# Layer 1's output projection in seven quarter products in place of eight, in a decoder step on one core

## The chip, the core and the metric

The kernel is one launch on one core of a Trainium2 chip. The core has five engines that each work through an instruction list of their own, in order: TensorE (PE: matmuls and transposes), VectorE (DVE), ScalarE (ACT), GpSimd (POOL) and SyncE (SP, which issues most of the DMAs). They wait for one another by semaphores. The metric is the device time of the launch in microseconds, the median of several runs; lower is better.

## The reference

One inference step of a trunk with two layers: 1040 prompt tokens (16 meta tokens and 1024 more) and 8 sample tokens, model width 1024, fp32. Layer 0 mixes by gated linear attention, layer 1 by differential attention over 8 heads of width 128; behind each mixer stand an output projection, a residual with a layer norm, an MLP of hidden width 4096 with a squared ReLU, and a residual with a layer norm again. What the change touches is the end of layer 1's mixer:

```
def post_norm(x, f, g, b):
    return layer_norm(DEEPNORM_ALPHA * x + f, g, b)

def diff_output(o, g_sub, lam_init, w_out, dtype):
    B, T = o.shape[:2]
    o = rms_norm(o, g_sub) * (1.0 - lam_init)
    return o.reshape(B, T, DIFF_HEADS * DIFF_DV).astype(dtype) @ w_out

def sq_relu_mlp(x, w1, w2):
    h = jax.nn.relu(x @ w1)
    return (h * h) @ w2
```

That is, a matrix of 1024 tokens x 1024 head columns times w_out (1024 x 1024), added to the residual stream, normalized, and given to the MLP. The meta and sample tokens go a small separate way.

## The kernel before

**Products in fp32.** An fp32 operand is split in two parts, hi and lo (`split`, L202 a cast on ACT, L203 a subtraction on DVE), and a product is three matmuls, hi x hi, lo x hi, hi x lo (`mm3`, L206 to L208). The parts of weights are named whi and wlo, those of tokens XH and XL, or two XH buffers. Weight parts come from a load into raw, rw or RW, a cast on ACT and a subtraction on POOL (L193 and L194, or L1585 and L1586).

**Layer 1's attention and w_out.** The attention writes each head's output into Y (tokens x columns). The "back" of a head transposes probabilities (L1318), copies them (ACT L1320), multiplies with the values (L1323), and evicts (ACT L1412). When four token tiles of a head are done and scaled (L1337), `o_fm` transposes them on PE (L1343) and makes the parts XH (ACT L1344) and XL (DVE L1345) of the features-first operand. As those heads finish, their space in Y is loaded with the scaled residual (`Y<-xres`, L1442, eight loads on SP). `w_out` then goes through 4 units of 256 output columns x 8 token tiles; each tile sums 8 k x 3 matmuls of 256 columns, two tiles to a PSUM bank, and DVE adds a bank to Y (L1022). Some of this work fills gaps of the attention's tail.

**Statistics and norm.** `normalize` takes the tiles that w_out yields: statistics (DVE L1045), their sum (L1049, L1053), a power on POOL (L1054), the shift (DVE L1058), and the scaled copy on ACT (L1060). After four tiles `to_fm` transposes them (PE L1071) and evicts them, scaled by the norm's weights, into XR (DVE L1075, ACT L1077), the MLP's tokens. The residual of the MLP, Y times a constant times ln_mix_g, is made by L1700 from `grow`, a row that lies in the buffer RP (load L1453).

**The MLP of layer 1.** Its up and down products are already in the seven-product form of quarters, once for each quarter g of the hidden width. `chip_operand` makes a token operand: a difference of two quarters where the table says so (DVE L1560 into RX), then the splits, into one of two XH buffers in turn. `weight_operand` makes a weight operand: loads (SP L1582), for a difference an accumulating DMA from POOL's queue (L1584), cast and subtraction. `up_tile` adds tiles of 258 columns into HF, `down_tile` tiles of 512 columns into RP (the running sum, L1659 and a copy L1663) and Y (L1659). The tables UP_X, UP_W, DOWN_H and DOWN_W say which quarters enter a product; "run" is the operand of an earlier product, still in RX or RW, carried on.

**What sets the order.** The program's text is not the order of the engines. The tile framework places each engine's instructions by a modelled timeline, in the priority of the program's text, and sets the semaphores. So an edit can move instructions that it doesn't name, and each engine then keeps that list at run time, whatever comes late.

Of the kernel before, what the change touches and what calls it, by code (L numbers as in the profile page):

```python
# [11 lines left out]
F32 = mybir.dt.float32  # L12
# [9 lines left out]
P = 128  # L22
D = 1024
# [91 lines left out]
def hybrid_step(ctx, tc, A, dbg=None, upto=9):  # L115
# [1222 lines left out]

    def o_fm(h, c):
        cs = slice(512 * c, 512 * c + 512)  # L1340
        ps = axt()
        for i in range(4):
            TE.transpose(ps[:, i * P : (i + 1) * P], Yt[:, 4 * c + i, h * P : (h + 1) * P], ident)  # L1343
        S.activation(XH[:, h, cs], ps, AF.Copy, scale=gs)  # L1344
        V.scalar_tensor_tensor(XL[:, h, cs], ps, gs, XH[:, h, cs].bitcast(F32), ALU.mult, ALU.subtract)  # L1345
# [106 lines left out]
    grow = RP[:, 0:2, :].rearrange("p a n -> p (a n)")  # L1452
    dma(grow, A["ln_mix_g"][1:2].broadcast_to([P, D]))  # L1453

# [35 lines left out]

    stats = ln_stats(hp)
    normalize(w_out(A["diff_w_out"][0], True, samples()), stats, lambda c: to_fm(c, 2, xr))
# [48 lines left out]

    count = [0, 0]
    loads = []
    sides = []

    def chip_operand(terms, quarter, n, tmp):


        parts = [x.rearrange("p k n -> p (k n)")[:, : 4 * n] for x in XH.t[count[0] % 2]]
        count[0] += 1  # L1550
        hi, lo = (x.rearrange("p (k n) -> p k n", n=n) for x in parts)
        rv, tv = (x[:, : 4 * n].rearrange("p (k n) -> p k n", n=n) for x in (RX, tmp))
        for j in (0, 2):
            b = slice(j, j + 2)
            x = quarter(*terms[0])[:, b]
            if len(terms) > 1:

                y = rv[:, b] if terms[1] == "run" else quarter(*terms[1])[:, b]
                out = (tv if terms[1] != "run" else rv)[:, b]
                V.tensor_tensor(out, x, y, op=ALU.subtract)  # L1560
                x = out
            split(hi[:, b], lo[:, b], x)
        return hi, lo

    def weight_operand(terms, quarter, side=None):

        hi, lo = (wsp.tile([P, 2048], F32R, name=n).rearrange("p (k n) -> p k n", n=512) for n in ("whi", "wlo"))
        run = terms[0] == "run"
        own = []

        def src(q, k):
            w, r0, c0 = quarter(*q)
            return w[r0 + k * P : r0 + (k + 1) * P, c0 : c0 + 512]

        for k in range(4):
# [171 lines left out]
```

## Time and profile before

| | us |
|---|---|
| median of 3 runs | 2814.77 |
| the runs | 2809.8 to 2817.36 |
| profiled execution, its time | 2803.96 |
| profiled execution, its span | 2802.2 |

In the profiled execution the granted TensorE clock was 0.993 of full speed, and 1.00 in the stages spoken of here. PE is busy 2715.8 us of the span, 97%. Rows of a timeline have the start, the duration, the engine, the line, the operation and its operands (out<-in); in brackets behind it stands how long the engine was idle before, and what released it. Durations of matmuls overlap, so their spacing is read from the starts. In a row of a group the numbers behind the bar are the busy time of the group, the mean of one in ns, and the idle time ahead of it. Windows are in us from the start of the span.

### The profile page before, as it was taken

To read this page: it belongs to the slowest core of one execution; us is meant where nothing else is said; L and a number is where in the kernel's file an instruction comes from. 1 tells how busy PE (TensorE), PEld (TensorE's weight loads), DVE (VectorE), ACT (ScalarE), POOL (GpSimd) and SP (SyncE) were. 2 spreads that over 40 slices of the span, in tenths; PEclk is the share of its full clock that TensorE was granted. 3 is DMA by queue.
4 is the path that set the end of the run, shared out by engine and by line. 5 is a ranking of instruction groups with operands and counts; after the bars stand their busy time and mean duration, and the time that the engine had idled before them with its cause. 6 is when DMAs were issued, how large, how long until landed. Compare 5 with 4: busy or idle time off the path is not lost.

```text
span 2802.2 us, 52241 instructions
## 1 busy us (share of the span) xinstructions
PE 2715.8 (97%) x19849; PEld 2233.8 (80%) x19849; DVE 1954.0 (70%) x3045; ACT 1096.4 (39%) x2233; POOL 1105.1 (39%) x744
## 2 busy tenths in 40 slices
PE   8988999999999999999999999999999999999997
PEld 5866767987777777777798988776899889797985
DVE  5466463668877777777677730887648888979788
ACT  4324363152231221221241112777535546355553
POOL 2142112243443343433234222100026677687774
PEclk9999999999999999999999999999999999999998
DMA  7565654735889898888658995122144455555584
GB/s 234 168 231 194 215 183 170 267 96 183 311 317 335 307 351 307 315 319 305 235 197 302 363 365 169 55 61 74 37 120 91 102 146 115 141 121 122 132 187 91
DMA packets 275624, 562.81 MB, mean 201 GB/s; under 512 B 23510, under 2 KB 144412, under 8 KB 271276
## 3 DMA queue, kind: packets, MB, share of 16 engines
q1 hardware_dynamic: 256076, 522.75, 54.1%
q0 software_dynamic: 19296, 36.71, 8.1%
q8 instruction: 156, 2.56, 0.4%
q14 instruction: 96, 0.79, 0.1%
HBM read 533.00 MB, written 29.52 MB: 201 GB/s over the span
## 4 chain that ended last, share of the span: by engine, by line
PE 74%; DVE 8%; ACT 4%; DMA 3%; issue 2%; POOL 1%; SPq 0%; DVEq 0%; POOLq 0%; ACTq 0%
PE mmt L206 17%; PE mmt L207 17%; PE mmt L208 17%; PE smt L952 4%; PE axt L206 3%; PE axt L207 3%; PE axt L208 3%; PE smt L1323 2%; ACT as L1301 2%; DVE pg L911 1%; PE prt L1297 1%; DMA swt<-in_mlp_w 1%; PE axt L1318 1%; DMA rw<-in_mlp_w 1%; PE smt L686 1%
## 5 line engine op out<-in xcount | busy, mean ns | idle before, releaser
L194 POOL TENSOR_TENSOR wlo<-raw,whi 128x512 fp32r<-128x512 f32 x252 | 364.4, 1459 | 730.6 <-ACT whi L193 599.6
L206 PE MATMUL mmt<-whi,XH 128*128 128x256 f32 (+1 forms) x1760 | 524.6, 300 | 1.3 <-DVE ast L1299 0.9
L207 PE MATMUL mmt<-wlo,XH 128*128 128x256 f32 (+1 forms) x1760 | 522.2, 298 | 0.4 <-POOL wlo L194 0.4
L206 PE MATMUL mmt<-XH,whi 128*128 128x512 f32 (+1 forms) x1216 | 434.2, 358 | 6.6 <-DVE Y L1022 3.0
L208 PE MATMUL mmt<-XH,wlo 128*128 128x512 f32 (+1 forms) x1216 | 432.0, 356 | 0.0
L208 PE MATMUL mmt<-whi,XL 128*128 128x256 f32 x1536 | 431.7, 284 | 0.0
L193 ACT CAST whi<-raw 128x512 fp32r<-128x512 f32 x252 | 150.5, 620 | 579.3 <-PE mmt L208 189.6
L206 PEld LDWEIGHTS mmt<-whi,XH 128*128 128x128 f32 x1760 | 330.7, 189 | 39.1 <-issue 24.3
L912 DVE TENSOR_REDUCE sc<-pg 128x16 f32<-128x1024 f32 x256 | 308.2, 1211 | 70.5 <-POOL pg L911 68.1
L207 PEld LDWEIGHTS mmt<-wlo,XH 128*128 128x128 f32 x1760 | 332.2, 189 | 17.5 <-issue 6.8
L207 PE MATMUL mmt<-XL,whi 128*128 128x512 f32 x768 | 306.9, 400 | 0.0
L911 DVE TENSOR_TENSOR pg<-pg,qb 128x1024 f32<-128x1024 f32 x192 | 262.7, 1375 | 57.9 <-DMA pg<-in_cache_k 46.8
L208 PEld LDWEIGHTS mmt<-whi,XL 128*128 128x128 f32 x1536 | 288.3, 189 | 4.4 <-issue 3.8
L206 PEld LDWEIGHTS mmt<-XH,whi 128*128 128x128 f32 x1216 | 229.0, 189 | 50.8 <-issue 7.5
L911 POOL TENSOR_TENSOR pg<-pg,qb 128x1024 f32<-128x1024 f32 x64 | 165.4, 2585 | 253.1 <-DMA pg<-in_cache_k 168.4
L208 PEld LDWEIGHTS mmt<-XH,wlo 128*128 128x128 f32 x1216 | 229.4, 189 | 36.4 <-issue 3.7
L206 PE MATMUL mmt<-whi,HH 128*128 128x512 f32 x512 | 204.6, 401 | 4.9 <-DVE Y L1136 3.4
L208 PE MATMUL mmt<-whi,HL 128*128 128x512 f32 x512 | 203.9, 398 | 0.0
L207 PE MATMUL mmt<-wlo,HH 128*128 128x512 f32 x512 | 203.4, 397 | 0.0
L1586 POOL TENSOR_TENSOR wlo<-RW,whi 128x512 fp32r<-128x512 f32 x96 | 166.1, 1767 | 58.1 <-ACT whi L1585 58.0
L1586 POOL TENSOR_TENSOR wlo<-rw,whi 128x512 fp32r<-128x512 f32 x92 | 156.8, 1778 | 79.1 <-ACT whi L1585 78.8
L207 PEld LDWEIGHTS mmt<-XL,whi 128*128 128x128 f32 x768 | 145.2, 189 | 38.4 <-issue 7.2
(438 smaller groups left out, 5707.8 us busy)
## 6 DMA issues: line engine op xcount, KB each, us to landing
pg<-in_cache_k SPq DMA_DIRECT2D x256, 512.0 KB
pg<-in_cache_v SPq DMA_DIRECT2D x256, 512.0 KB
raw<-in_mlp_w SPq DMA_DIRECT2D x164, 256.0 KB
swt<-in_mlp_w SPq DMA_DIRECT2D x32, 1024.0 KB
rw<-in_mlp_w SPq DMA_DIRECT2D x116, 256.0 KB
RW<-in_mlp_w POOLq DMA_DIRECT2D x96, 256.0 KB, 5.8
swt<-in_gla_w_in SPq DMA_DIRECT2D x12, 1024.0 KB
swt<-in_diff_w_in SPq DMA_DIRECT2D x12, 1024.0 KB
```

The costliest lines, as they stand in the source:

```text
L193: S.copy(hi[:, c], raw)
L194: G.tensor_tensor(lo[:, c], raw, hi[:, c].bitcast(F32), op=ALU.subtract)
L206: TE.matmul(ps, ah, bh, start=first, stop=False)
L207: TE.matmul(ps, ah, bl, start=False, stop=False)
L208: return TE.matmul(ps, al, bh, start=False, stop=last)
L686: TE.matmul(ps[o : o + TS, :], lhs[:, k + 2 * j + i, :], ts[j][:, i, c * 512 : (c + 1) * 512], start=k == 0 and j == 1, stop=k == nk - 4 a ...
L911: eng.tensor_tensor(pg, pg, qb, op=ALU.mult)
L912: return V.tensor_reduce(sc[:, n, :], pg.rearrange("p (h d) -> p h d", d=64), op=ALU.add, axis=AX.X).ins
L952: m = TE.matmul(acc[i * TS : i * TS + 16, :256], w[r, n, :], pg[r, i * 256 : (i + 1) * 256], start=n == 0, stop=n == NPG).ins
L1301: S.activation(sc_[:, m, :W], sc_[:, m, :W], AF.Exp, bias=mns[:, m : m + 1], scale=-1.0, accum_out=l[:, m : m + 1])
L1323: TE.matmul(out, at, v, start=j == 0, stop=j == t + 1)
L1586: G.tensor_tensor(lo[:, k, :], t, hi[:, k, :].bitcast(F32), op=ALU.subtract)
```

## The change

`w_out` of layer 1 becomes `w_out_1`: seven products of quarters (512 tokens or columns a side) in the order 1, 2, 5, 6, 3, 7, 4, by the tables DOWN_H and DOWN_W that the MLP's down product uses, with `chip_operand`, `weight_operand` and `down_tile`, which move up in the text for it. Each product has 4 token tiles, each of 4 k x 3 matmuls of 512 columns, so 336 matmuls stand for 768. `o_fm` keeps whole fp32 columns, OF0 and OF1, with one eviction for each four tiles (ACT for even heads, DVE for odd ones); the parts are made by `chip_operand`. The first two products' weights use the buffers raw alone. RP now holds running sums of w_out, so the load of `grow` into it moves behind w_out. Layer 0's w_out stays as it was. The line numbers shift: L1346 is the heads' transpose now, L1447 the residual's load, L1511 the difference, L1536 to L1540 the weights, L1558 and L1562 the sums and the copy of `down_tile`, L1702 the load of grow, and L1732 the multiplication that was L1700.

```diff
     def o_fm(h, c):
-        cs = slice(512 * c, 512 * c + 512)
+        if c == len(OF):
+            OF.append(cp.tile([P, NB, TH], F32, name="OF%d" % c, tag="XL%d" % c))
         ps = axt()
         for i in range(4):
             TE.transpose(ps[:, i * P : (i + 1) * P], Yt[:, 4 * c + i, h * P : (h + 1) * P], ident)
-        S.activation(XH[:, h, cs], ps, AF.Copy, scale=gs)
-        V.scalar_tensor_tensor(XL[:, h, cs], ps, gs, XH[:, h, cs].bitcast(F32), ALU.mult, ALU.subtract)
+        if h % 2:
+            V.tensor_scalar(OF[c][:, h, :512], ps, gs, None, ALU.mult)
+        else:
+            S.activation(OF[c][:, h, :512], ps, AF.Copy, scale=gs)
...
-    grow = RP[:, 0:2, :].rearrange("p a n -> p (a n)")
-    dma(grow, A["ln_mix_g"][1:2].broadcast_to([P, D]))
...
     def weight_operand(terms, quarter, side=None):
...
+        plain = len(seen) < 2
+        seen.append(0)
...
             if run or (len(terms) > 1 and terms[-1] != "new"):
                 t = RW[:, k, :]
             else:
                 count[1] += 1
-                t = wrp.tile([P, 512], F32, name="raw") if count[1] % 7 in (0, 3) else rawt()
+                t = wrp.tile([P, 512], F32, name="raw") if plain or count[1] % 7 in (0, 3) else rawt()
...
+    def w_out_1():
+
+        side = samples()
+        wo = A["diff_w_out"][0]
+
+        def operands(i):
+            left = chip_operand(DOWN_H[i], lambda c, k: OF[c][:, 4 * k : 4 * k + 4, :512], 512, RX)
+            return left, weight_operand(DOWN_W[i], lambda k, u: (wo, 512 * k, 512 * u))
+
+        seq = (1, 2, 5, 6, 3, 7, 4)
+        nxt = operands(seq[0])
+        n = 0
+        for at, i in enumerate(seq):
+            now = nxt
+            for t in range(4):
+                if t == 1 and at + 1 < len(seq):
+                    nxt = operands(seq[at + 1])
+                n += 1
+                down_tile(0, i, t, *now, axt() if n % 2 else mmt())
+                if i == 5 and t == 0:
+                    next(side)
+                for c, u in {3: [(0, 0), (0, 1)], 7: [(1, 1)], 4: [(1, 0)]}.get(i, ()):
+                    yield 4 * c + t, u
+
     stats = ln_stats(hp)
-    normalize(w_out(A["diff_w_out"][0], True, samples()), stats, lambda c: to_fm(c, 2, xr))
+    normalize(w_out_1(), stats, lambda c: to_fm(c, 2, xr))
...
+    grow = RP[:, 0:2, :].rearrange("p a n -> p (a n)")
+    dma(grow, A["ln_mix_g"][1:2].broadcast_to([P, D]))
+
     def mlp1():
```

Three places in the engines' lists. First DVE around the end of w_out, before: L1022 adds w_out's last banks, L1700 multiplies the residual, L203 with XH_23783 and then with XH_24052 splits the operands of the MLP's first two products, L1075 evicts XR.

```order
L203 TENSOR_TENSOR XH_23783<-XR_24892,XH_84 128x1032
L1700 SCALAR_TENSOR_TENSOR Y<-Y,RP 128x1024 x3
L1075 TENSOR_SCALAR XR_24892<-axt,lnp 128x512
L1700 SCALAR_TENSOR_TENSOR Y<-Y,RP 128x1024
L1022 TENSOR_TENSOR Y<-Y,mmt 128x2x256
L1045 BN_STATS bst<-Y 128x6 x2
L1049 BN_AGGR bmv<-bst 128x2 x2
L1053 TENSOR_SCALAR brs<-bmv 128x2
L203 TENSOR_TENSOR XH_24052<-XR_24892,XH_86 128x1032
L1058 SCALAR_TENSOR_TENSOR brs<-bmv,brs 128x2
L203 TENSOR_TENSOR XH_24052<-XR_24892,XH_86 128x1032
L1022 TENSOR_TENSOR Y<-Y,mmt 128x2x256
```

And the same place now; L1558 on RP and then twice on Y is a tile of product 7, L1558 on Y from axt a tile of product 4, the last; the splits of the MLP's first product go into XH_24045, those of its second into XH_23783.

```order
L1558 TENSOR_TENSOR RP<-RP,axt 128x512
L203 TENSOR_TENSOR XH_24045<-XR_24633,XH_86 128x1032
L1558 TENSOR_TENSOR Y<-Y,RP 128x512 x2
L1732 SCALAR_TENSOR_TENSOR Y<-Y,RP 128x1024 x4
L1558 TENSOR_TENSOR Y<-Y,axt 128x512
L1045 BN_STATS bst<-Y 128x6
L203 TENSOR_TENSOR XH_23783<-XR_24633,XH_84 128x1032
L1558 TENSOR_TENSOR Y<-Y,axt 128x512
L203 TENSOR_TENSOR XH_23783<-XR_24633,XH_84 128x1032
L1045 BN_STATS bst<-Y 128x6 x2
```

The four multiplications stood ahead of w_out's last two sums, directly behind the splits of the MLP's first product; now all four stand together between product 7 and product 4, directly ahead of the rows that the second product needs.

Second, SP behind the attention, now. Y<-xres are the residual's loads, each behind the heads that lie in its place; RW<-in_diff_w_out the weights of product 5, rw<-in_diff_w_out those of later ones.

```order
L1447 DMA Y<-xres 128x4x256 x4
L1489 DMA rw<-srow 128x512
L1087 DMA ht<-in_ln_mix_b 128x256
L1447 DMA Y<-xres 128x4x256 x2
L1465 DMA sx<-sxd 128x256
L154 DMA c_inv<-in_cf 128x128
L1447 DMA Y<-xres 128x4x256
L1536 DMA RW<-in_diff_w_out 128x512 x3
L1447 DMA Y<-xres 128x4x256
L1536 DMA RW<-in_diff_w_out 128x512
L1536 DMA rw<-in_diff_w_out 128x512 x6
```

Before, ten of w_out's sixteen weight loads were issued ahead of all these rows, and RP<-in_ln_mix_g stood among the residual's loads; now the ten ahead are those of products 1 and 2 and one each of 3 and 7, and product 5's stand behind seven of the eight residual loads.

Third, PE at the last head of the attention, now. L1323 multiplies by the values, L1346 transposes finished heads, the mmt rows are w_out's product 2.

```order
L1323 MATMUL smt<-XA_21036,aT 128x128 x3
L1346 MATMUL axt<-c_ident,Y 128x128 x4
L1323 MATMUL smt<-XA_21036,aT 128x128 x2
L1346 MATMUL axt<-c_ident,Y 128x128 x8
L208 MATMUL mmt<-whi,XH_24045 128x512
L206 MATMUL mmt<-whi,XH_86 128x512
L207 MATMUL mmt<-wlo,XH_86 128x512
```

Before, w_out's matmuls of 256 columns stood between the rows of the last heads too, 155 of them in the last 43 us of the attention; now 26 of 512 columns stand ahead of the last heads, and the rest behind them.

125 lines of the change are left out of this document (63 added, 62 removed).

## The prediction

> **What bounds the kernel now.** I read the page first (time, busy shares), then a table of the stages, then the waits at their edges. This kernel's runs spread from 2809.8 to 2817.36 us, 0.27%, so I take 0.3% (8.4 us) as the least difference that a measurement tells from none.
>
> ```profile
> span 2802.2 us, 52241 instructions
> PE 2715.8 (97%) x19849; PEld 2233.8 (80%) x19849; DVE 1954.0 (70%) x3045; ACT 1096.4 (39%) x2233; POOL 1105.1 (39%) x744
> ...
> core 0: us, PE busy (x) PEld busy (x) DVE busy (x) ACT busy (x) POOL busy (x), PEclk, DMA share, GB/s
> 2035.00:2118.90 83.90, 80.90 (x689) 80.69 (x687) 47.75 (x80) 27.79 (x43) 29.86 (x22) 1.00 0.39 114
> 2118.90:2204.70 85.80, 82.52 (x680) 81.38 (x681) 68.66 (x90) 52.47 (x99) 55.87 (x44) 1.00 0.47 98
> 2204.70:2287.20 82.50, 82.50 (x370) 63.40 (x369) 75.68 (x70) 35.40 (x56) 59.34 (x44) 1.00 0.60 140
> ```
>
> The first stretch is layer 1's w_out, the second the first quarter of the up product of the MLP behind it, the third that quarter's down product, which already has the seven-product form that the change brings to w_out. PE is busy 80.90 of 83.9 us in w_out, VectorE only 47.75: TensorE sets this stage, with much slack beside it. In the third stretch VectorE works 75.68 of 82.5. That is the question of this change: it takes work from the engine that is full and gives work to one that would then be nearly full. The edge of w_out shows what PE waits for there:
>
> ```profile
> 2112.86 0.28 PE L206 MATMUL mmt<-XH,whi 128*128 128x258 f32 x1
> ...
> 2118.91 0.39 PE L206 MATMUL mmt<-XH,whi 128*128 128x258 f32 x1 [3.01 <-DVE Y L1022]
> ```
>
> PE leaves w_out at 2112.86, begins the MLP, and then stands 3.01 us for operands that VectorE is late with.
>
> **TensorE's part.** w_out was 4 units x 8 token tiles x 8 k x 3 = 768 matmuls of 256 columns; now 7 products x 4 tiles x 4 k x 3 = 336 of 512. Their spacing is read in two stretches without a gap (of 70 rows in w_out, of 36 in a down product, the first and the last):
>
> ```profile
> 2069.73 0.28 PE L207 MATMUL mmt<-wlo,XH 128*128 128x256 f32 x1
> ...
> 2077.88 0.28 PE L207 MATMUL mmt<-wlo,XH 128*128 128x256 f32 x1
> ...
> 2699.71 0.39 PE L206 MATMUL mmt<-whi,XH 128*128 128x512 f32 x1
> ...
> 2707.81 0.40 PE L208 MATMUL axt<-whi,XH 128*128 128x512 f32 x1
> ```
>
> 8.15 us by 69 is 0.118; 8.10 by 35 is 0.231. So 768 x 0.118 = 90.7 becomes 336 x 0.231 = 77.7: **13 us less of PE**, all that can be won; the multiplications saved are an eighth, 11.3, and the wide form gives the rest. Transposes stay in number.
>
> Where this shows: before, 155 of the matmuls filled the tail of the attention, whose last rows come out at 2032.72.
>
> ```profile
> L206 PE MATMUL mmt<-whi,XH 128*128 128x256 f32 x52 | 14.6, 288 | 1.1 <-DVE ast L1299 0.9 <-ACT XH L1344 0.2
> L207 PE MATMUL mmt<-wlo,XH 128*128 128x256 f32 x52 | 14.4, 284 | 0.0
> L208 PE MATMUL mmt<-whi,XL 128*128 128x256 f32 x51 | 13.3, 293 | 0.0
> ...
> 2032.72 0.58 ACT L1412 COPY Y<-smt 128x512 f32<-128x512 f32 x1 [3.47 <-PE smt L1323]
> ...
> 2032.52 1.04 PE L1343 MATMUL axt<-c_ident,Y 128*128 128x128 f32 x8
> ```
>
> By the order, only 26 of the new ones stand in that tail (6.0 us for 18.3), so the attention ends 12.3 us sooner, X = 2020.4. From X, PE has 310 x 0.231 = 71.6, sixty transposes at 0.12 (1.04 for the eight of the last row above, the latency of one in it) and a few small ones, together 79.3: were nothing in the way, w_out would end at 2099.7, 13 before 2112.86.
>
> **VectorE's part.** Its rows in w_out before, and then the same forms in the two nearest stretches of seven products, the first quarter's down (2204.7 to 2287.2) and the last one's (2707 to 2802):
>
> ```profile
> L1045 DVE BATCH_NORM_STATS2 bst<-Y 128x6 f32<-128x512 f32 x14 | 9.0, 685 | 0.2
> L1022 DVE TENSOR_TENSOR Y<-Y,mmt 128x512 f32<-128x512 f32 x13 | 8.9, 684 | 25.9 <-PE mmt L208 25.9
> L1700 DVE SCALAR_TENSOR_TENSOR Y<-Y,RP 128x1024 f32<-128x1024 f32 x4 | 7.8, 1988 | 0.5 <-PE axt L1071 0.5
> L1345 DVE SCALAR_TENSOR_TENSOR XL<-axt,gs,XH 128x512 fp32r<-128x512 f32 x7 | 5.1, 731 | 0.7 <-ACT XH L1344 0.5
> L203 DVE TENSOR_TENSOR XH<-XR,XH 128x1032 fp32r<-128x1032 f32 x4 | 4.9, 1229 | 1.5 <-ACT XH L202 1.5
> L1075 DVE TENSOR_SCALAR XR<-axt,lnp 128x512 f32<-128x512 f32 x4 | 3.2, 807 | 2.2 <-PE axt L1071 2.0
> ...
> L203 DVE TENSOR_TENSOR XH<-RX,XH 128x1024 fp32r<-128x1024 f32 x8 | 17.0, 2120 | 1.1 <-ACT XH L202 1.1
> L1659 DVE TENSOR_TENSOR Y<-Y,RP 128x512 f32<-128x512 f32 x12 | 10.1, 872 | 0.1
> L1560 DVE TENSOR_TENSOR RX<-HF,RX 128x1024 f32<-128x1024 f32 x4 | 7.5, 1867 | 0.0
> L1560 DVE TENSOR_TENSOR RX<-HF 128x1024 f32<-128x1024 f32 x3 | 4.6, 1556 | 0.0
> ...
> L203 DVE TENSOR_TENSOR XH<-RX,XH 128x1024 fp32r<-128x1024 f32 x5 | 9.4, 1881 | 0.5 <-ACT XH L202 0.5
> L203 DVE TENSOR_TENSOR XH<-HF,XH 128x1024 fp32r<-128x1024 f32 x4 | 6.4, 1589 | 5.0 <-ACT XH L202 5.0
> L203 DVE TENSOR_TENSOR XH<-XR,XH 128x1024 fp32r<-128x1024 f32 x2 | 2.4, 1213 | 0.0
> L1659 DVE TENSOR_TENSOR Y<-Y,RP 128x512 f32<-128x512 f32 x12 | 13.0, 1111 | 0.2
> ```
>
> The same instruction has two prices: a split's subtraction 1.21 us undisturbed, 1.6 to 2.1 where GpSimd's subtractions run beside it. One place shows it raw:
>
> ```profile
> 2229.81 2.32 POOL L1586 TENSOR_TENSOR wlo<-raw,whi 128x512 fp32r<-128x512 f32 x1
> 2231.08 3.56 POOL L1586 TENSOR_TENSOR wlo<-rw,whi 128x512 fp32r<-128x512 f32 x2
> ...
> 2230.38 6.59 DVE L203 TENSOR_TENSOR XH<-RX,XH 128x1024 fp32r<-128x1024 f32 x1
> ...
> 2103.36 6.21 DVE L1700 SCALAR_TENSOR_TENSOR Y<-Y,RP 128x1024 f32<-128x1024 f32 x3 [0.48 <-PE axt L1071]
> ...
> L194 POOL TENSOR_TENSOR wlo<-raw,whi 128x512 fp32r<-128x512 f32 x8 | 10.6, 1334 | 15.7 <-ACT whi L193 15.7
> ```
>
> One subtraction took 6.59 us while GpSimd worked through its own. The Trainium skill ("SBUF — State Buffer", section "SBUF: two separate sides") says that VectorE instructions with two SBUF inputs and GpSimd's exclude one another for a whole instruction, the loser being blocked; the trace agrees (1.21 against 6.59). It speaks against this change, which replaces sums out of PSUM by differences and splits out of SBUF and raises GpSimd's subtractions for w_out from 16 to 28.
>
> From X to the MLP's entry VectorE now has, disturbed (undisturbed in brackets): 8 differences for products 5, 6, 3 and 7 at 1.73, the mean of the L1560 rows, 13.9 (1.21: 9.7); 14 splits, ten for these and product 4 and four for the MLP's first two, at 1.65, the mean of the last quarter's L203 rows, 23.1 (1.21: 16.9); 30 sums out of PSUM at 0.68, 20.4; 12 sums Y<-Y,RP at 0.99, between their two rows, 11.9 (0.68: 8.2); 13 statistics at 0.685, 8.9; 4 evictions at 0.81, 3.2; 3 or 4 new evictions of heads, 2.6; what is left of the 47.75 once the six quoted groups are taken off, 8.9. **Together 92.9 (78.8)**, where PE has 79.3. About 6 us of it come after PE's last w_out matmul, so VectorE allows the end of w_out at X + 73 to X + 87; by the L203 and L1560 stretches it idles a few us more for ScalarE's casts (1.1 in one row, 5.0 in another; 5.6 taken). So PE ends w_out between 2099.7 and 2113; I take the middle, 2106.4: **6.5 us gained of the 13.**
>
> **The entry into the MLP.** The diff loads ln_mix_g into RP behind w_out, since RP now holds a product. The four multiplications L1700 ran inside w_out before (the 6.21 row and one more); now they stand, as L1732, between product 7's last sums and product 4's, and ahead of the splits for the MLP's second product. Behind PE's end VectorE needs about 0.6, the four L1732 (4 x 1.22 = 4.9 if undisturbed, 4 x 2.07 = 8.3 by that row), two sums and one statistics at 0.68, and two splits: 10 to 14.2 us. The MLP's first product covers 48 x 0.12 = 5.8. So PE stands 4.2 to 8.4 there. The next step, 32 transposes of tiles 4 to 7, needs their statistics and ScalarE's normalization, four of the following:
>
> ```profile
> L1060 ACT ACTIVATE Y<-Y,brs 128x1024 f32<-128x1024 f32 x6 | 7.1, 1235 | 14.4 <-DVE brs L1058 14.4
> ```
>
> 4.9 us and as much for what precedes it, covered by the 5.8 us of the MLP's second product but for 0 to 4.6. Together 4 to 13, 8.5 in the middle, for the 3.0 before: **5.5 us lost.** The load of ln_mix_g itself is issued when product 7's tile 0 is summed, some 7 us of VectorE work ahead of L1732; I cost it at nothing; a late one would lengthen this gap by as much as it is late. It waits on SP for product 7's first sums, and behind it there wait the loads for the MLP's third product, which PE needs only some 17 us later.
>
> **Taken as nothing.** The heads' transposes: one eviction each in place of a cast and a subtraction (0.731, row L1345), on engines that are not the bound then. Weights: DMA share is 0.39 in w_out. GpSimd: its rows stay under the 59.34 of 82.5 it works in the third stretch; were this cover gone, a late weight costs one 1.3 to 2.3 us subtraction at a product's start.
>
> **Sum.** -6.5 + 5.5 = -1 us, against the profiled run's 2803.96, which lies 10.8 under the median; carried to the median, 2814.
>
> **Rivals.** (a) *PE sets the stage and the gain stays.* For it: in the third stretch the same code keeps PE at 82.50 of 82.5 with VectorE at 75.68. Against it: there VectorE has no statistics, evictions and sample rows beside it. It decides if VectorE's work is near 79. Then -13.2, and an entry at its low end, +1: 2803. (b) *VectorE and GpSimd exclude one another and w_out lasts longer.* For it: the 6.59. Work of 92.9 with its idling already puts the end at 2113 (+0.1), and with an entry of 13 (+10) the kernel is at 2825. If each of the 24 subtractions for products 5 to 4 and the MLP's first two cost VectorE its own 1.33 (row L194), the undisturbed 78.8 would become 111, the end 2020.4 + 111 - 6 = 2125.4 (+12.5), with the middle entry 2833. It decides from VectorE work of about 95 on. Against it: the two stretches of before never reached that. The Trainium skill's rule of exclusion, taken at its word for every pair, would make it the 2833, an estimate. (c) *Product 5's weights are late.* On SP they are queued behind seven of the eight loads Y<-xres, which wait for the heads' transposes:
>
> ```profile
> SPq L1442 <- PE axt L1343: 8.4, 3, 4.1
> ...
> RW<-in_mlp_w POOLq DMA_DIRECT2D x96, 256.0 KB, 5.8
> ```
>
> These transposes end about 6 us behind X, product 5 begins about 20 behind X. Loads, an accumulating DMA (5.8 us by the median of such issues), a cast and a subtraction take 17 to 22 in all: at most 4 us, 2818, no change as measured.
>
> **How the numbers follow.** My forecast 0.40 and (c) 0.07 lie within 0.3% of before, (a) 0.30 is faster, (b) 0.23 slower. So faster 0.30, same 0.47, slower 0.23; forecast 2814, alone 2806 to 2822. The range reaches to (a)'s 2803 less 2 and well into (b): 2801 to 2830.
>
> **What would show it.** PE's matmuls 0.231 apart; the attention's last L1323 near 2020; w_out's last matmul between 2100 and 2113 and VectorE busy over 95% of the stage (under 90% speaks for (a)); VectorE splits over 2 us on average for (b); L1732 ahead of the splits with PE waiting 4 to 8 us for XH behind the MLP's first product. It is wrong if PE waits in w_out for weights or PSUM banks rather than for VectorE's operands, or if the up and down products of the MLP change by more than 2 us.

## The result: 0.9% slower

| | before | after |
|---|---|---|
| median of 6 runs, us | 2809.7 | 2836.97 |
| the runs, us | 2805.78 to 2817.36 | 2831.47 to 2842.34 |
| profiled execution: time, span, clock | 2803.96, 2802.2, 0.993 | 2831.47, 2829.7, 0.987 |

The kernel before has three more runs here than in the table ahead of the change. The ratio after to before is 1.0092, with a 95% interval of 1.0074 to 1.0111. By the bound of 0.3% the kernel is slower; the forecast was no change, 2814 us, and the range ended at 2830.

TensorE does have less to do: its matmuls of w_out are 336, spaced 0.231 us. The time went elsewhere. The view of the stretches, of the profile after, with the columns of the same view before. Rows one and two are w_out and the MLP's first up product (quarter 0); the last two are the down product of quarter 1 and the up product of quarter 2:

```profile
2035.00:2122.20 87.20, 76.38 (x324) 58.20 (x323) 79.25 (x104) 35.98 (x49) 52.02 (x43) 0.96 0.57 129
2122.20:2226.20 104.00, 91.62 (x705) 88.46 (x704) 82.42 (x101) 57.27 (x105) 64.80 (x49) 0.93 0.43 92
2226.20:2308.80 82.60, 82.60 (x371) 63.48 (x370) 77.13 (x70) 35.36 (x57) 56.79 (x44) 1.00 0.59 137
...
2389.20:2474.20 85.00, 83.25 (x370) 63.12 (x369) 77.14 (x67) 36.12 (x57) 57.04 (x44) 1.00 0.56 131
2474.20:2560.40 86.20, 83.77 (x672) 83.37 (x673) 65.29 (x82) 49.63 (x97) 63.57 (x45) 0.96 0.49 106
```

Of the profile before, the last two stretches:

```profile
2367.70:2450.90 83.20, 82.91 (x371) 63.41 (x370) 76.48 (x70) 35.40 (x57) 58.12 (x44) 1.00 0.59 141
2450.90:2531.30 80.40, 80.40 (x673) 80.40 (x672) 60.76 (x79) 50.28 (x97) 61.82 (x44) 1.00 0.51 106
```

VectorE in w_out rose from 47.75 us to 79.25, and TensorE is no longer full: 76.38 of 87.2, at a clock of 0.96. The spans differ by 27.5 us, and the marks between the stages divide them (to 0.1 us):

| part | before | after | difference | forecast |
|---|---|---|---|---|
| up to the first L1323 of layer 1's attention | 1761.2 | 1762.0 | +0.8 | 0 |
| from there to the end of w_out | 351.7 | 360.2 | +8.5 | -6.5 |
| up product, quarter 0 | 91.9 | 104.0 | +12.2 | +5.5 |
| down 0 and up 1 | 163.0 | 163.0 | 0 | 0 |
| down 1 and up 2 | 163.6 | 171.2 | +7.6 | 0 |
| down 2 and up 3 | 163.0 | 163.0 | 0 | 0 |
| down 3 and the end | 107.9 | 106.3 | -1.6 | 0 |

Three places lose. What TensorE waits for at the first two is the view of its waits between 1990 and 2250 (what waits, for what: us in total, times, the longest), of the profile after:

```profile
PE mmt L207 <- DVE XH L203: 6.2, 1, 6.2
PE mmt L206 <- DVE Y L1558: 4.0, 2, 3.4
PE mmt L206 <- DVE RP L1558: 3.0, 2, 2.3
PE axt L206 <- DVE HF L1679: 2.9, 1, 2.9
PE axt L1071 <- ACT Y L1060: 2.8, 5, 0.6
...
PE axt L1346 <- ACT OF L1350: 1.8, 1, 1.8
...
PE mmt L208 <- POOL wlo L1540: 0.3, 1, 0.3
```

Three quarters of it is VectorE, 19.6 of 26.0 us: operands (XH), and sums that free a PSUM bank (Y and RP, L1558; HF, where before had 2.8 too). ScalarE has 6.1, weights 0.3. Before, the whole view comes to 7.9 us. And VectorE is late because single instructions of it take long while GpSimd subtracts. VectorE's and GpSimd's timelines at one such place, and VectorE's at the MLP's entry:

```profile
2065.37 3.16 DVE L1511 TENSOR_TENSOR RX<-OF,OF 128x1024 f32<-128x1024 f32 x1
2068.46 6.27 DVE L203 TENSOR_TENSOR XH<-RX,XH 128x1024 fp32r<-128x1024 f32 x1
2074.66 0.18 DVE L735 TENSOR_TENSOR sv__24361<-sv__24361,sy__24362 128x32 f32<-128x32 f32 x1
2074.77 1.22 DVE L1511 TENSOR_TENSOR RX<-OF,OF 128x1024 f32<-128x1024 f32 x1
...
2067.64 2.27 POOL L1540 TENSOR_TENSOR wlo<-rw,whi 128x512 fp32r<-128x512 f32 x1
2069.66 1.49 POOL L1540 TENSOR_TENSOR wlo<-raw,whi 128x512 fp32r<-128x512 f32 x1
2070.92 2.72 POOL L1540 TENSOR_TENSOR wlo<-rw,whi 128x512 fp32r<-128x512 f32 x2
...
2122.92 8.97 DVE L1732 SCALAR_TENSOR_TENSOR Y<-Y,RP 128x1024 f32<-128x1024 f32 x4
2131.82 0.67 DVE L1558 TENSOR_TENSOR Y<-Y,axt 128x512 f32<-128x512 f32 x1
2132.42 0.68 DVE L1045 BATCH_NORM_STATS2 bst<-Y 128x6 f32<-128x512 f32 x1
2133.02 2.31 DVE L203 TENSOR_TENSOR XH<-XR,XH 128x1032 fp32r<-128x1032 f32 x1
```

The difference L1511 takes 1.22 us where GpSimd doesn't subtract and 3.16 where it does; the split behind it takes 6.27 and ends 1.1 us behind GpSimd's run of four (2070.92 + 2.72 = 2073.6), about what a split takes undisturbed. A sum out of PSUM (`Y<-Y,axt`) takes 0.67 at either time. The four L1732 are such a place too: GpSimd subtracts for the MLP's weights beside them, and they take about 2.3 us each, where the other four, at 2152 to 2158 and without GpSimd, take 1.2.

A further cost, which lies within these parts, is TensorE's clock. Windows of 5 us of the profile after at the entry, and TensorE's timeline behind the wait of 6.16 us:

```profile
2130.00:2135.00 5.00, 0.00 (x0) 0.00 (x0) 5.00 (x4) 0.00 (x0) 5.00 (x4) 0.76 0.43 134
2135.00:2140.00 5.00, 4.62 (x23) 4.62 (x24) 3.37 (x6) 0.00 (x0) 1.36 (x3) 0.56 0.83 161
2140.00:2145.00 5.00, 3.92 (x31) 3.35 (x29) 2.15 (x9) 2.87 (x3) 1.80 (x3) 1.00 0.45 65
2145.00:2150.00 5.00, 3.40 (x16) 2.65 (x16) 2.35 (x3) 3.21 (x4) 0.00 (x0) 0.62 0.00 0
2150.00:2155.00 5.00, 4.98 (x30) 4.58 (x29) 4.90 (x6) 1.93 (x3) 0.00 (x0) 0.70 0.01 2
...
2135.38 0.58 PE L207 MATMUL mmt<-XH,whi 128*128 128x258 f32 x1 [6.16 <-DVE XH L203]
2135.76 0.42 PE L208 MATMUL mmt<-XH,wlo 128*128 128x258 f32 x1
...
2139.20 0.37 PE L208 MATMUL mmt<-XH,wlo 128*128 128x258 f32 x1
```

Sixteen spacings from 2135.76 to 2139.20 are 0.215 us each, where this form otherwise has 0.12. Summed over windows of 1 us (busy time by the missing share of the clock), the lower clock took 12.3 us between 1985 and 2600 after, and none before; 5.0 of them lie between 2110 and 2160, beside 9.3 us of idle time (3.5 before).

### The profile page after: what moved, and what is told of

Same layout as the page of the kernel before. It is cut to its first block, busy times and chain, and to the rows that moved or that the text cites. A ratio compares the mean times of both kernels' runs of the same rounds, so it can differ in the third digit from the quotient of the medians.

```text
span 2829.7 us, 51518 instructions
## 1 busy us (share of the span) xinstructions
PE 2720.8 (96%) x19417; PEld 2213.9 (78%) x19417; DVE 2010.7 (71%) x3087; ACT 1113.6 (39%) x2255; POOL 1136.4 (40%) x772
## 4 chain that ended last, share of the span: by engine, by line
PE 69%; DVE 11%; ACT 4%; DMA 4%; issue 3%; POOL 1%; SPq 0%; DVEq 0%; POOLq 0%; ACTq 0%
PE mmt L206 16%; PE mmt L207 16%; PE mmt L208 16%; PE smt L952 4%; PE axt L206 3%; PE axt L207 3%; PE axt L208 3%; PE smt L1323 2%; DVE Y L1558 2%; ACT as L1301 2%; DVE XH L203 1%; DVE pg L911 1%; DMA swt<-in_mlp_w 1%; PE prt L1297 1%; PE axt L1318 1%
## 5 line engine op out<-in xcount | busy, mean ns | idle before, releaser
L194 POOL TENSOR_TENSOR wlo<-raw,whi 128x512 fp32r<-128x512 f32 x236 | 345.9, 1479 | 699.3 <-ACT whi L193 558.5
L206 PE MATMUL mmt<-whi,XH 128*128 128x256 f32 (+1 forms) x1560 | 477.6, 308 | 7.3 <-DVE Y L1558 4.0
L207 PE MATMUL mmt<-wlo,XH 128*128 128x256 f32 (+1 forms) x1560 | 474.8, 305 | 0.4 <-POOL wlo L194 0.4
L208 PE MATMUL mmt<-whi,XL 128*128 128x256 f32 x1280 | 362.2, 284 | 0.0
L193 ACT CAST whi<-raw 128x512 fp32r<-128x512 f32 x236 | 140.7, 619 | 558.5 <-PE mmt L208 181.3
L206 PEld LDWEIGHTS mmt<-whi,XH 128*128 128x128 f32 x1560 | 294.3, 189 | 49.6 <-issue 28.5
L207 PEld LDWEIGHTS mmt<-wlo,XH 128*128 128x128 f32 x1560 | 295.8, 190 | 20.1 <-issue 7.2
L208 PEld LDWEIGHTS mmt<-whi,XL 128*128 128x128 f32 x1280 | 241.9, 189 | 4.4 <-issue 3.8
L1540 POOL TENSOR_TENSOR wlo<-RW,whi 128x512 fp32r<-128x512 f32 x108 | 183.1, 1739 | 76.6 <-ACT whi L1539 76.5
L1540 POOL TENSOR_TENSOR wlo<-rw,whi 128x512 fp32r<-128x512 f32 x97 | 167.2, 1810 | 61.8 <-ACT whi L1539 61.7
```

Source lines behind the costliest of these rows:

```text
L193: S.copy(hi[:, c], raw)
L194: G.tensor_tensor(lo[:, c], raw, hi[:, c].bitcast(F32), op=ALU.subtract)
L206: TE.matmul(ps, ah, bh, start=first, stop=False)
L207: TE.matmul(ps, ah, bl, start=False, stop=False)
L208: return TE.matmul(ps, al, bh, start=False, stop=last)
L1540: G.tensor_tensor(lo[:, k, :], t, hi[:, k, :].bitcast(F32), op=ALU.subtract)
```

## Experiments

Ratios are to the kernel before on the same chip, with their 95% intervals. Where executions of variants are compared, it is the length of a stage, since their starts of w_out lie up to 13 us apart. "w_out" is, for the seven-product kernels, the stretch from its first matmul to its last, 118.0 us with the change; "up 0" is the up product of quarter 0, 104.0. Each length is of one execution: in the variants that leave w_out as the change has it (e3, e6, e7, e9, e12, e13) it takes 114.0 to 117.8, and in those that leave the entry alone (e1, e2, e5, e7, e13) up 0 takes 103.2 to 106.5.

**e1: without GpSimd's subtractions in w_out.** TensorE takes the weights' hi part for their lo part, so that part of the product is left out and replaced.

```diff
-            G.tensor_tensor(lo[:, k, :], t, hi[:, k, :].bitcast(F32), op=ALU.subtract)
+            if sub:
+                G.tensor_tensor(lo[:, k, :], t, hi[:, k, :].bitcast(F32), op=ALU.subtract)
...
-            return left, weight_operand(DOWN_W[i], lambda k, u: (wo, 512 * k, 512 * u))
+            return left, weight_operand(DOWN_W[i], lambda k, u: (wo, 512 * k, 512 * u), sub=False)
```

> Left out: GpSimd's 28 subtractions for the weights of w_out (the hi part stands in for lo), so the product's numbers are not the reference's; every matmul, load, cast and VectorE instruction of w_out stays. The changed kernel has 2837 us; in its profile w_out ends on TensorE at 2122.2 and VectorE's splits and sums beside GpSimd take up to 6.3 and 9.0 us. Theory A (VectorE is the bound of w_out because it and GpSimd shut one another out): VectorE's splits in w_out fall to 1.2 us, w_out ends 10 to 15 us sooner, at about 2108 to 2112, and the kernel takes 2822 to 2827. Theory B (VectorE's own amount of work is too much even undisturbed): the end moves by less than 5 us, 2832 or more. Theory C (weights arrive late behind the residual's loads on SP): the end moves by 1 to 3 us, a GpSimd step less in each product's chain, 2834.

Measured: 2819.31 us, 1.0026 (1.0013 to 1.0039), a little more gained than theory A's 2822 to 2827. w_out takes 102.9 us in place of 118.0. The window of w_out, three groups of VectorE in it, and the last four of the sums Y<-Y,RP, in pairs:

```profile
2035.00:2103.80 68.80, 68.11 (x313) 55.32 (x312) 61.59 (x99) 35.78 (x49) 20.92 (x22) 1.00 0.67 151
...
L1559 DVE TENSOR_TENSOR Y<-Y,RP 128x512 f32<-128x512 f32 x12 | 10.1, 869 | 0.1
L203 DVE TENSOR_TENSOR XH<-RX,XH 128x1024 fp32r<-128x1024 f32 x8 | 9.8, 1220 | 3.2 <-ACT XH L202 3.2
...
L1559 DVE TENSOR_TENSOR Y<-Y,mmt 128x512 f32<-128x512 f32 x12 | 7.9, 679 | 1.0 <-PE mmt L208 1.0
...
2096.39 1.30 DVE L1559 TENSOR_TENSOR Y<-Y,RP 128x512 f32<-128x512 f32 x2
...
2101.08 3.50 DVE L1559 TENSOR_TENSOR Y<-Y,RP 128x512 f32<-128x512 f32 x2
```

The same groups with the change:

```profile
L203 DVE TENSOR_TENSOR XH<-RX,XH 128x1024 fp32r<-128x1024 f32 x8 | 17.2, 2155 | 3.3 <-ACT XH L202 3.3
L1558 DVE TENSOR_TENSOR Y<-Y,RP 128x512 f32<-128x512 f32 x12 | 12.7, 1082 | 0.1
...
L1558 DVE TENSOR_TENSOR Y<-Y,mmt 128x512 f32<-128x512 f32 x12 | 7.9, 679 | 0.8 <-PE mmt L208 0.7
```

Splits out of SBUF fall from 2.16 to 1.22 us, sums of two SBUF operands from 1.08 to 0.87, sums out of PSUM stay at 0.68. The 0.87 is a mean of two prices: ten of the twelve take 0.68 or 0.69, and the last two, beside which GpSimd subtracts for the MLP's weights, 1.79 each. TensorE is full again, at clock 1.00. The entry keeps its 6.1 us wait (up 0 is 103.2).

**e5: the subtractions run, but nobody reads them.** As e1, but GpSimd still subtracts. This tells the engines' exclusion from a chain through GpSimd's results.

```diff
-        return hi, lo
+        return hi, lo if used else hi
...
+            return left, weight_operand(DOWN_W[i], lambda k, u: (wo, 512 * k, 512 * u), used=False)
```

> As e1 for the numbers (hi stands in for lo in w_out's weights, so they are not the reference's), but GpSimd still does all 28 subtractions; nobody waits for their results. It parts the two ways in which e1 could have gained its 18 us. Theory A1 (GpSimd's work itself stretches VectorE's): as the changed kernel, 2832 to 2840, with splits of 2 us and more in w_out. Theory A2 (TensorE waited for late lo parts, a longer chain for each weight): as e1, 2816 to 2823, with GpSimd busy and no wait of TensorE in w_out.

Measured: 2833.09 us, 1.0076 (1.0049 to 1.0103); w_out 118.1, up 0 104.3. No matmul of w_out waits for GpSimd (for the hi parts from ScalarE they wait 1.2 us in all), and the loss is all there: it is the subtractions' running beside VectorE, not their results being late. The load buffers still wait for GpSimd to have read them, which this run doesn't take away; the 1.2 us is all that TensorE waits for weights.

**e2: without the eight differences.** Products 5, 6, 3 and 7 take the first quarter in place of a difference of two; the second one is left out.

```diff
-            left = chip_operand(DOWN_H[i], lambda c, k: OF[c][:, 4 * k : 4 * k + 4, :512], 512, RX)
+            left = chip_operand(DOWN_H[i][:1], lambda c, k: OF[c][:, 4 * k : 4 * k + 4, :512], 512, RX)
```

> Left out: the eight differences of token quarters in w_out (each product takes the first quarter alone), so the numbers are not the reference's; splits, sums, weights and matmuls stay. Theory A and theory B (VectorE sets the stage): 8 instructions of 1.2 to 3.2 us less on the bound, together 14 us: w_out's end 10 to 14 us sooner and 2823 to 2827. Theory C (late weights): less than 4 us, 2833 or more.

Measured: 2832.41 us, 1.0074 (1.0048 to 1.0101); w_out 114.9, 3.1 us shorter, up 0 103.3. Theory A and B's 10 to 14 us didn't come; 3.1 us is within what w_out varies by. The number is theory C's, but in this run's w_out TensorE doesn't wait for weights at all. The differences dropped were 12.8 us (6.0 + 4.4 + 2.4, VectorE's L1511 groups); VectorE's busy time in w_out fell by 8.5, from 95.2 to 86.7, and its idle time rose by 5.3. The 14 splits kept their price, 24.8 us for 25.0, one of them 5.61 beside a run of GpSimd's subtractions. So it is not VectorE's sum of work alone that sets the end.

**e3 and e6: L1732 later.** The four multiplications go behind the splits for the MLP's second product (e3), or each behind the last split ahead of it in the text, and so singly (e6).

```diff
...
-                        steps_v.append(V.scalar_tensor_tensor(y, y, ALPHA, grow, ALU.mult, ALU.mult).ins)
+                        with tc.issue_after(splits[17]):     (e3; e6: splits[-1])
+                            steps_v.append(V.scalar_tensor_tensor(y, y, ALPHA, grow, ALU.mult, ALU.mult).ins)
```

> Order alone: the four multiplications of tiles 0 to 3 by ln_mix_g are placed behind the splits of the MLP's second product. In the changed kernel they took 8.97 us there, TensorE stood 6.16 us for the split behind them and ran its next 4 us at a lower clock. Theory D (their place costs what the wait shows): the wait falls under 1 us, 6 to 8 us gained, 2830. Theory E (the norm of tiles 4 to 7 is the next in line and now comes behind the multiplications): the wait moves to the transposes L1071 and 0 to 3 us are gained, 2834 to 2837.

> Order alone: each of the eight multiplications by ln_mix_g is placed behind the newest split of an MLP operand, so from the third product of the MLP on, past the norm of tiles 4 to 7. The changed kernel's first up quarter takes 104.0 us from its first to its last product (91.9 before); e3, which only put them behind the second product's splits, 103.2, since their 8.94 us then held up the statistics. Theory D2 (they are what the entry lacks, on the chain of the norm): 94 to 97 us for the quarter and 2827 to 2830 for the kernel. Theory I (the entry is held by w_out's own end, where all four tiles 4 to 7 are finished last): the quarter stays over 99 us, 2832 or more.

Measured: e3 2833.66 us, 1.0076 (1.0051 to 1.0101), up 0 103.2; e6 2828.3 us, 1.0065 (1.0043 to 1.0087), up 0 96.1. In e3 the splits are in time, but the four still stand in one run, now ahead of the statistics of tiles 4 to 7 (the last line is of TensorE's waits):

```profile
2133.92 8.94 DVE L1733 SCALAR_TENSOR_TENSOR Y<-Y,RP 128x1024 f32<-128x1024 f32 x4
2142.78 0.20 DVE L1049 BATCH_NORM_AGGREGATE bmv<-bst 128x2 f32<-128x12 f32 x1
...
PE axt L1071 <- ACT Y L1060: 4.6, 5, 3.1
```

The wait of 6.2 us is gone, but those for the norm grew from 2.8 to 4.6 and those for weights from 0.3 to 2.4, and up 0 is as long as before the edit. Spread out (e6), up 0 falls to 96.1 (96.2 in e9 and 97.1 in e11 and e14, which have the same order), and the clock stays up; in the time, e6's interval still meets the change's. The window of the entry:

```profile
2110.00:2160.00 50.00, 45.69 (x322) 41.06 (x321) 35.48 (x48) 29.26 (x46) 25.87 (x18) 1.00 0.30 75
```

**e12: TensorE kept busy at the entry.** Eighteen matmuls 128 x 512 more behind each of the MLP's first two products, read by nobody.

```diff
+                    if g == 0 and at < 2 and t == 3:
+                        fill = mmt()
+                        (ah, _), (bh, _) = now
+                        for j in range(18):
+                            TE.matmul(fill, ah[:, j % 4, 0:P], bh[:, j % 4, 0:512], start=True, stop=True)
```

> The changed kernel with 36 matmuls more, 128 x 512, whose results nobody reads: 18 behind the MLP's product 1 and 18 behind its product 2 of quarter 0, where TensorE stood 6.2 us and then in shorter waits. Theory K (the granted clock falls because TensorE has gaps, and not because of what VectorE and GpSimd do there): the clock stays near 1.00 between 2110 and 2160, the 5.0 us that the lower clock took there are gone, the added 8.3 us (36 x 0.231) lie mostly in the 9.3 us of idle time, and the stretch from the end of w_out to the first matmul of down's quarter 0 goes from 104.0 to 99-104 us; 2828-2837 us in all. Its rival: the clock falls there in any case, or the added matmuls add their own time; then that stretch is 108-112 us and the time 2840-2846 us.

Measured: 2831.88 us, 1.0066 (1.0037 to 1.0095); up 0 102.7. The entry's window, of e12 and then of the change:

```profile
2110.00:2160.00 50.00, 46.17 (x287) 40.97 (x286) 38.43 (x44) 22.31 (x34) 22.33 (x14) 0.97 0.27 69
```
```profile
2110.00:2160.00 50.00, 40.65 (x243) 36.23 (x244) 38.48 (x43) 21.17 (x32) 19.90 (x14) 0.86 0.27 69
```

VectorE's work is the same (38.43 and 38.48), and the clock rises from 0.86 to 0.97: its loss falls from 5.0 us to 1.6. So most of the lower clock follows TensorE's gaps. The 8.3 us of added matmuls fit into gaps and regained clock. That time was gained is not shown: up 0 is 0.5 us under the shortest of the variants without them.

**e4, e8, e10: the wide form without the saved product.** Eight products of quarters, 384 matmuls of 512 columns (88.7 us by 0.231), no difference anywhere. e4 keeps the new fp32 columns; e8 makes the heads' parts as before the change; e10 is e8 with two buffers for the rows of ln_mix_b (below).

```diff
-        seq = (1, 2, 5, 6, 3, 7, 4)
+        seq = ((0, 0, 0), (0, 0, 1), (0, 1, 1), (0, 1, 0), (1, 1, 0), (1, 1, 1), (1, 0, 1), (1, 0, 0))
...
+                yv = Yt[:, 4 * c + t, 512 * u : 512 * u + 512]
+                steps_v.append(V.tensor_tensor(yv, yv, ps, op=ALU.add).ins)
```

> Eight quarter products of 512 columns in place of seven: no differences, no running sum, 384 matmuls, whole fp32 columns and their splits as in the change, each output tile summed by VectorE from PSUM (64 tile sums). TensorE 384 x 0.231 = 88.9 us, 11 more than the change and 2 less than before. Theory A or B (VectorE's surplus work makes the loss): with about 25 us less work on VectorE no wait in w_out is over 1 us, and the kernel takes 2806 to 2812, as before or a little less. Theory F (the wide form with whole columns itself is what costs, by a later end of the attention and a worse entry): 2820 or more.

> As e4 (eight quarter products of 512 columns), but the heads are made into hi and lo parts as they are evicted, as before the change, so no whole columns and no splits in w_out. What is left of the change is the matmul's width, with 32 sums of 128x512 on VectorE in place of 16. Theory F1 (in e4 the whole columns cost: TensorE stood 1.8 us for an eviction and ran on at a lower clock, and the heads were finished later): 2805 to 2811, before or up to 4 us less. Theory F2 (the wide form costs, by the quarter that must be complete before its first product): as e4, 2815 to 2819.

> e8 with two buffers for the same rows. Its profile has the same late row (quarters of 84.9 and 86.3). Theory J: 6 to 8 us less than e8, 2806 to 2808, so level with the kernel before or up to 3 us better. Rival: as e8, 2814.

Measured: e4 2817.19 us, 1.0033 (1.0016 to 1.005); e8 2814.08 us, 1.0023 (1.0009 to 1.0038); e10 2815.82 us, 1.0014 (1.0001 to 1.0026). Up 0 is 88.1 in e4 and e8, shorter than before's 91.9, so the long entry belongs to the seven products and not to the move of the row or the wide form. In e8 the longest wait for a head's eviction is 0.7 us (1.3 in three), and no clock was lost up to 2110; with the change (and in e4) TensorE waits 1.8 us for that eviction (`L1346 <- ACT OF L1350`), and the clock falls behind it. e4's time lies between the ranges of its theories, and so does e8's, so the times don't decide between F1 and F2; e10's is not theory J's. None of the three beats the kernel before.

**e7, e9: the loss in quarters 1 and 2.** e7 sets the buffers' counters, which w_out now shares with the MLP, back to zero; e9 is e6 with two buffers for the rows of ln_mix_b, one of which came late at the end of down 1 (a wait of 3.10 us of VectorE for it, 2.55 before).

```diff
+    count[:] = [0, 0]      (e7, ahead of mlp1)
...
-    ht = e.enter_context(tc.tile_pool(name="ht", bufs=HTB))
+    ht = e.enter_context(tc.tile_pool(name="ht", bufs=2))      (e9, with e6's edit)
```

> The counters that choose the token buffers and the weight buffers are set back to zero between w_out and the MLP, so that the MLP starts with the buffers it had before the change. In the changed kernel's profile the MLP's second down quarter took 85.0 us and its third up quarter 86.2, before 83.1 and 80.5: 7.7 us far behind w_out. Theory G (the shifted rotation of the buffers causes these): both go back, 6 to 8 us gained, 2829 to 2831. Theory H (they come from something else, as an order of the loads that differs anyhow): less than 2 us, 2835 or more.

> e6, and the rows of ln_mix_b for the MLP's residual get two buffers in place of one, so that a row's load doesn't wait for the row before it. In the changed kernel and in e5 to e8 VectorE stood about 3 us for such a row at the end of the second down quarter, directly ahead of the splits for the next up quarter; TensorE then waited 4 us and went on at a lower clock. Theory J (that load, moved behind by the reordered lists, makes the 7.7 us far behind w_out): second down quarter and third up quarter together go from 171 back to 164, 6 to 8 us less than e6: 2821 to 2823. Rival (the sums and splits of that place are late without it): less than 2 us, 2827.

Measured: e7 2834.78 us, 1.0093 (1.0075 to 1.0111), down 1 and up 2 170.2 us: not the counters. e9 2828.93 us, 1.0066 (1.0043 to 1.0088), against e6's 2828.3 no gain: down 1 and up 2 fall from 170.2 to 166.5 us, but up 1 grows from 80.5 to 84.7. The stall moved and stayed as large, which is the rival's number. e8, whose up 0 and down 0 are no longer than before's, has the same two long quarters as the change (84.9 and 86.3), so they don't need a MLP that starts late.

**e11, e13, e14: GpSimd out of the way, place by place.** e11 joins e1, e6 and the two row buffers. e13 is the change without GpSimd's subtractions for the weights of quarters 1 and 2 alone. e14 is both together. TensorE takes the hi part for the lo part of the weights where GpSimd doesn't subtract: those of w_out in e11, of quarters 1 and 2 in e13, of both in e14.

```diff
-            left = weight_operand(UP_W[i], lambda h, k: (w1, 512 * k, 1024 * g + 512 * h))
+            left = weight_operand(UP_W[i], lambda h, k: (w1, 512 * k, 1024 * g + 512 * h), sub=g not in (1, 2))
...   (and the same for DOWN_W)
```

> e1 (GpSimd's 28 subtractions for w_out left out, so the numbers are not the reference's), e6's order of the multiplications and e9's two row buffers together. If the three places are all that the change loses, their gains add up: 18 + 9 + 7 off 2837 is 2803, some 6 us under the kernel before, which is about half of the 13 us that TensorE saves. If they overlap (a wait removed at one place comes back at the next): 2810 or more.

> The changed kernel without GpSimd's subtractions for the weights of the MLP's quarters 1 and 2 (TensorE takes the high halves for the low ones there); w_out and quarter 0 as in the change. Theory L (the far loss is made by VectorE and GpSimd shutting each other out in those quarters): up, down and up of quarters 1, 1 and 2, 251.7 us with the change and 244.1 before, take 243-245 us; 2836 - 8 = 2826-2831 us in all. Its rival (a late row of ln_mix_b, shifted lists or TensorE's clock make the far loss, whatever GpSimd does): those three stay at 250-252 us, 2833-2838 us.

> As e11 (no subtractions of w_out's weights on GpSimd, multiplications behind the splits, two buffers of rows), and without GpSimd's subtractions in the MLP's quarters 1 and 2. Theory L, and with it that the 13 us are there once the exclusion is gone at all places: the three stretches take 243-245 us, 252.9 in e11, and the time is 2812 - 8 = 2801-2805 us, faster than before by 0.2-0.4%. Its rival: the far loss stays or turns up again behind, 2809-2813 us.

Measured: e11 2812.02 us, 1.0005 (0.999 to 1.002), level with before and 9 us above what was expected, because up 1, down 1 and up 2 took 252.9 us there. e13 2828.11 us, 1.0052 (1.0034 to 1.007). e14 2804.51 us, 0.9977 (0.9961 to 0.9992), faster than before. The three stretches, of e13:

```profile
2313.50:2394.00 80.50, 80.50 (x674) 80.50 (x673) 49.12 (x79) 50.49 (x97) 14.23 (x16) 1.00 0.52 109
2394.00:2476.50 82.50, 82.50 (x370) 63.38 (x370) 59.64 (x73) 34.93 (x57) 14.24 (x16) 1.00 0.60 142
2476.50:2556.90 80.40, 80.40 (x673) 80.40 (x672) 45.62 (x76) 50.39 (x97) 14.25 (x16) 1.00 0.50 106
```

TensorE is full in all of them: 243.4 us, where the change has 251.7 and before 244.1. The count of VectorE's instructions is about the same (73 and 67 in down 1), but its busy time there falls from 77.14 to 59.64. The twelve variants that keep these subtractions take 245.2 to 253.3 us there; only e13 and e14 come back to 243.4 and 243.5. And with the change no matmul waits for GpSimd in these quarters, all waits are for VectorE (down 1 and up 2):

```profile
PE axt L207 <- DVE XH L203: 2.4, 2, 1.2
PE axt L206 <- DVE Y L1558: 1.7, 1, 1.7
```

So the loss in quarters 1 and 2 goes with the same subtractions as that in w_out. In e13's profile the last quarter's down product was longer by 6.5 us than with the change (waits for sums in RP, 2.9, and for weights, 2.7), so its span (2832.7) doesn't show the gain that its median does; why that quarter differed wasn't tried.

## Why the prediction was wrong

**Right.** TensorE's saving of 13 us: the spacing of 0.231, the 336 matmuls, and e14, once GpSimd was out of the way at w_out and in two quarters. From the attention's first L1323 to the end of w_out e14 takes 342.6 us, 9.1 less than before, and there are 3.5 us in it for a head's eviction (below), 12.6 together. As a whole e14 is 7.1 us under the 2811.6 before; its up 0 is still 5.2 us longer. The kernel before wasn't run without its own subtractions, so 7.1 is no measure of the change alone; its trace leaves them 0.6 us at most in the three stretches of quarters 1 and 2 (244.1 against 243.5), and the wait of 3.0 at the edge of w_out. VectorE's sum: 92.9 us forecast from the attention's last row to the second split of the MLP. Measured over that stretch, less the 8.97 of L1732, 94.1:

```profile
2024.30:2137.10 112.80, 94.27 (x438) 73.75 (x437) 103.07 (x127) 45.65 (x73) 66.50 (x52) 0.95 0.58 140
```

The terms are off by up to 3.0 and even out: the 14 splits took 26.1 for 23.1, the eight differences 12.8 for 13.9. The place of L1732 ahead of the splits, PE's wait of 4 to 8 us there (6.2) and the price of over 2 us for the eight splits out of RX (2.16) came as said. Weights of product 5 were not late (c).

**Wrong: the step "PE ends w_out between 2099.7 and 2113; I take the middle".** The two ends were two engines' lists, TensorE's and VectorE's, and a stage that needs both can't end before the later one, so it doesn't end between the two. With 92.9 us the later one was VectorE's, and the sum itself said 2113: the middle took 6.6 us off. From there to the measured 2122.2 it is 9.2 us more: attention's end 3.9 later (2024.3 against 2020.4), VectorE idle 9.7 us in place of 5.6 (112.8 - 103.07), and 1.2 more work. Neither engine was full: VectorE worked 88.2 of the 97.9 us from 2024.3 to 2122.2, 90%, not over 95%, and TensorE 85.9. They waited for one another in turn. TensorE's waits there were mostly of the kind that the prediction named as a sign against itself: 7.2 us for sums that free PSUM banks, 1.5 for operands. It is VectorE that was late with both. The row of 3.01 us in the kernel before, read as a wait for operands, is of the first kind too: it ended with the sum L1022, which frees the bank. That is rival (b), whose first reckoning gave 2825; its condition, VectorE work of about 95 on, wasn't even met (94.1). Its second reckoning, 2833, is the figure nearest to the measured 2837, but by luck: it takes VectorE's work as 111 us.

**Wrong: heads' evictions "taken as nothing".** One eviction costs TensorE a wait of 1.8 us and the clock 1.7 us behind it; e8, which has the old evictions, has neither. They make 3.5 of the 3.9. The 1.7 is not in every execution: e9 has the same wait of 1.8 us and kept its clock.

**Mis-sized: the entry.** Forecast 5.5 us lost, measured 12.2. The four L1732 took 8.97 for at most 8.3; the waits between 2110 and 2160 came to 9.3 us for 8.5. What was missing is the clock, 5.0 us there (0 before): the sum counted gaps and nothing for the time after them. The "0 to 4.6" in it doesn't follow from its own terms either (2 x 4.9 less 5.8 is 4.0), which moves the middle by 0.3.

**Missed: the MLP "by more than 2 us".** The prediction named this as a sign against it; it came to 7.6 us in quarters 1 and 2. The reason given for taking GpSimd's and VectorE's load in these stretches as harmless was that before shows TensorE full beside it. It was full with little to spare: VectorE had 76.48 of 83.2 us there. Without GpSimd's subtractions the loss is gone (e13, e14). Why the change's shifted lists run into them where those of before didn't stays open; the counters (e7), the late row alone (e9) and a late start of the MLP (e8) don't explain it.

**The skill's rule, which the prediction weighed.** The Trainium skill ("SBUF — State Buffer", section "SBUF: two separate sides") says that VectorE instructions with two SBUF inputs and GpSimd's lock each other out for a whole instruction. e1 and e5 bear it out for this kernel: splits with two SBUF operands, 2.16 us beside the subtractions (2.00 in e5) against 1.22 without them; one operand in PSUM, 0.68 both times; results read or not, no difference.

## What to carry to other kernels

A stage that two engines can bound ends no sooner than the longer of their lists: add up each with the prices it will have beside the other engines, take the maximum, take no mean, and add that engine's waits (here VectorE idled 9.7 us). On VectorE an instruction with two SBUF operands has two prices, alone and beside GpSimd; a change that moves work from TensorE to such instructions, and raises GpSimd's count as well, should be costed at the dear price from the start. And a gap of TensorE can cost more than its length, because of the clock behind it, so a burst on VectorE is better spread than moved.

## What was not expected of the hardware

TensorE's clock fell behind short gaps, but not behind each. With a wait of 1.8 us that ended at 2002.6 the granted clock was 0.79 in that window of 5 us and 0.87 in the next, while before the change a wait of 3.01 us (2115.9 to 2118.9) left it at 1.00. Windows of 3.41 us show why. In the traces the lower clock is one half, and it lasts 3.41 us or a multiple of it. Of the change, the window with the wait of 1.8 us and the next one:

```profile
1999.49:2002.90 3.41, 1.58 (x14) 1.08 (x13) 3.41 (x10) 3.38 (x9) 0.00 (x0) 0.99 0.45 154
2002.90:2006.31 3.41, 3.41 (x13) 2.64 (x12) 3.41 (x9) 3.41 (x10) 0.00 (x0) 0.51 0.48 153
```

Of the kernel before, the two windows that share the wait of 3.01 us, on the grid of its own lower clock:

```profile
2114.05:2117.46 3.41, 1.85 (x16) 1.65 (x14) 2.82 (x4) 1.50 (x4) 3.21 (x3) 1.00 0.00 0
2117.46:2120.87 3.41, 1.96 (x16) 1.96 (x17) 3.40 (x7) 2.80 (x5) 3.41 (x3) 1.00 0.32 94
```

TensorE was busy 46% of the window ahead of the fall, and 54% and 57% of the two that split the longer wait. e9's wait of 1.8 us also falls into two windows, with 53% in the first, and the clock stayed at 1.00. Over all sixteen traces, from 100 us on, the full clock fell behind every window in which TensorE was busy under 45% by the profile's modelled times, and of 173 falls one came behind a window of more than 57%; between the two it went either way. So what decides is a window that is about half idle, and where the gap lies in it.

The Trainium skill ("TensorE: Matmul & The Clock Gate", Part 1) has the half clock after an idle window of about 3.4 us that runs freely. The half rate agrees (0.215 against 0.12 us between matmuls), and so does the length; a gap of 1.8 us that lowers the clock does not agree with a fully idle window.
